# Large two-operand work moved from GpSimd to VectorE, and a new order in a mixer and in four layer norms

## The chip, the core and the metric

One core of a Trainium2 chip runs a forward pass of a small network in float32. Its engines are named as in the profile: PE (TensorE), with its weight loads as PEld, DVE (VectorE), ACT (ScalarE), POOL (GpSimd) and SP (SyncE, which here only issues DMAs). The metric is the device time of one execution in microseconds, lower is better.

## The reference

The input is one sequence of 256 tokens with 1024 features. The first block has two layers; each is a mixer, a layer norm, a SwiGLU feed-forward (1024 to twice 2816 and back) and a layer norm, with residuals. The second block has two layers with RMS norms: a half feed-forward, a mixer, a half feed-forward. The part around the change, cut:

```python
def layer_norm(x, g, b):
    mu = jnp.mean(xf, axis=-1, keepdims=True)
    xc = xf - mu
    var = jnp.mean(xc * xc, axis=-1, keepdims=True)
    return xc * lax.rsqrt(var + EPS) * g + b
...
for layer in range(DEPTH):
    ...   # mixer: layer 0 hgrn2 + forgetting attention, layer 1 rg_lru + stick-breaking attention
    x = layer_norm(ALPHA * x + mix, ln_g[layer, 0], ln_b[layer, 0])
    x = layer_norm(ALPHA * x + swiglu(x, ffn_w13[layer], ffn_w2[layer]), ln_g[layer, 1], ln_b[layer, 1])
```

The second block's mixers are an MLA with a dilated attention, and a sparse attention with a sliding-window one. Their logits get a position bias from a table, plus a mask.

## The kernel before, in words

The activations stay in SBUF with features on partitions. All weights pass once through the chip in **chunks** of 256 columns, in the fixed order of `chunk_plan` (L72): `fetch` (L429) issues the DMA of a chunk into `raw` on SP, ACT copies it to `wh` in a rounded format, and DVE makes `wl = raw - wh`, each in two halves of 128x1024. There are 3 `raw`, 4 `wh` and 4 `wl` buffers, so a chunk can be loaded only when an older one's `wl` is made. Activations are split in the same way into `ah` and `al`, and a product is three matmuls: `ah` with `wh`, `ah` with `wl`, `al` with `wh` (`steps_a` L484 gives features on partitions, `steps_b` L505 tokens on partitions). `chunk` (L447) keeps the next three chunks fetched.

In program order: mixer0 (to 143 us in the profile), layer norm 00 (to 174), feed-forward f0 (to 334), layer norm 01 (to 362), mixer1 (to 440), layer norm 10 (to 467), feed-forward f1 (to 626), layer norm 11 (to 655), then h0a (to 835), mixer2 (to 955), h0b (to 1140), h1a (to 1320), mixer3 (to 1430) and h1b.

In a mixer many small chains (attention heads, the levels of `level`, the gated recurrence `lru`) are generators; `weave` (L969) steps them in the order written out in the table `ORDER` (L36), a name per step. Within that a scheduler places the instructions on each engine's own in-order queue. In the layer norms the order is the program's (`manual_schedule`). In mixer0 each of eight `level`s (128 down to 1) makes a 128x1024 tile by two subtractions of 128x512 from the cumulated gates, one by DVE and one by POOL, an exponential on ACT, and two multiplications, again one by DVE and one by POOL.

`ln` (L592) overlaps the norm with the next stage: the un-normalised `x` is already multiplied with the next two weight chunks (`product`), and `first` (L726) corrects the results afterwards. `tail` (called per pair of 128-row blocks) sums x and its squares, `apply` (L735) gets mean and variance from PE, adds minus the mean to x, makes a diagonal of the reciprocal deviations (`dg`), broadcasts it by a matmul with ones (`row`), multiplies x by it, and makes `ah` and `al` of the next stage. `rms` (L794) sums squares in `tot`. In `ffn` (L851), `up` makes gate and up products of a chunk pair and `down` adds the result's share; `LAG` (L59) says by how many pairs `down` trails `up`. `t5_bias` (L1477) loads a bias by SP from a table in DRAM and adds a mask that POOL's queue has loaded. `mixer1.lru` starts with a convolution on DVE.

Every operation of ACT, DVE and POOL is recorded at L337, matmuls at L468, transposes at L481.

Of the kernel before, what the change touches and what calls it, by code (L numbers as in the profile page):

```python
# [12 lines left out]
def _quiet(msg, *args, **kwargs):  # L13
# [11 lines left out]
OP = mybir.AluOpType  # L25
# [12 lines left out]
        qb0 lv16 kb0 lv32 lv64 lv16 lv4 lv1 lv64 qb1 lv128 lv128 kb0 qb0 lv0 qb1 vb0 vb1 lv32 lv1 lv16 kb1 forget lv4  # L38
        lv64 ia0 ia0 fox1 vb0 lv8 lv8 lv0 fox0 vb1 fox1 lv2 lv32 lv1 kb1 fox2 fox3 lv128 fox3 ia1 ga0 ia1 fox1 fox0
        lv2 fox2 ga0 ga1 lv8 fox0 ga1 lv2 lv4 hgrn fox3 fox2 fox0 hgrn hgrn fox2 fox3 fox1 evo0 hgrn evo0 evo0 evo1  # L40
# [18 lines left out]
LAG = {"h0a": 2}  # L59
# [12 lines left out]
def chunk_plan():  # L72
# [25 lines left out]
    for name, c in (("fa", 512), ("qa", 0), ("qb", 2048), ("kb", 2560), ("vb", 3072),  # L98
                    ("ia", 1024), ("ga", 1536)):
        cols(name, "ev_w_in", c, 2)  # L100
# [250 lines left out]
class Net:  # L351
# [132 lines left out]
    def steps_a(s, w, act, n=256, parts=((0, 128), (128, 128))):  # L484
# [4 lines left out]
        for low in range(2):  # L489
            for k in range(8):  # L490

                js = range(len(parts)) if not low or k < 7 else range(len(parts) - 1, -1, -1)
                for j in js:
                    c0, m = parts[j]
                    p, c = o[:m, j * 256:(j + 1) * 256], slice(c0, c0 + m)
                    if low:
                        s.mm(p, h[:, k, c], al[:, k], False, k == 7 and j == 0)
                    else:
                        s.mm(p, h[:, k, c], ah[:, k], k == 0 and j == 0, False)
                        s.mm(p, l[:, k, c], ah[:, k], False, False)  # L500
# [91 lines left out]
    def ln(s, name, ahead=(), gain=None):  # L592
# [79 lines left out]
        def tail(pr, acc):  # L672
# [4 lines left out]
            if pr == 1:  # L677
# [19 lines left out]
            if pr == 3:  # L697
                with manual(ENG.PE):
# [17 lines left out]
                    for n in range(2):  # L716
                        product(n, range(6, 8), low=False)
# [17 lines left out]
        def apply():  # L735
# [21 lines left out]
            for pr in range(2, 4):  # L757
                nc.gpsimd.tensor_tensor(xs[pr], xs[pr], wide(nm), OP.add)
# [1303 lines left out]
```

## Time and profile before

| | us |
|---|---|
| runs timed, median (lowest to highest of 3) | 1635.88 (1635.45 to 1637.84) |
| profiled execution, its own time | 1634.74 |
| its span in the trace | 1633.0 |
| PE busy in the span | 1578.3 (97%) |
| DVE busy | 1098.9 (67%) |
| ACT busy | 850.8 (52%) |
| POOL busy | 214.8 (13%) |
| granted TensorE clock, mean | 0.991 |

The span runs from the first to the last instruction. A matmul's end is modelled and overlaps the next one, so idle time of PE is better read as the wait that the trace puts ahead of an instruction. [...]

### The profile page before, as it was taken

The page shows a single profiled execution, that of the slowest core. Times are in us where ns is not written, and L with a number is a line of the kernel's source. Part 1 is how long each engine was busy: PE and PEld are TensorE (multiplying, and loading weights), DVE is VectorE, ACT ScalarE, POOL GpSimd, SP SyncE. Part 2 cuts the span into 40 slices and gives each one's busy share as a digit, 9 for nine tenths or more (in the row PEclk, how much of TensorE's full clock was granted, in tenths as well). Part 3 has the DMA queues.
Part 4 walks back from the last instruction along what each step waited for, and adds up shares of the span by engine and source line. Part 5 has one row for each costly group of instructions (what it writes and reads, how often), then busy time and mean ns, then how long its engine had stood idle before and what let it go on. Part 6 is the DMA issues. An engine that isn't in the chain of part 4 may idle for free.

```text
span 1633.0 us, 31856 instructions
## 1 busy us (share of the span) xinstructions
PE 1578.3 (97%) x13635; PEld 1537.8 (94%) x13635; DVE 1098.9 (67%) x1683; ACT 850.8 (52%) x1271; POOL 214.8 (13%) x185
## 2 busy tenths in 40 slices
PE   8899999998999999999999999999999999899998
PEld 7798999988999998999999899999999998699998
DVE  7687845499795457856566865556756578775554
ACT  6474644467664445534366754444444456664442
POOL 6313100041120003100033210000000033110000
PEclk9999999999999999999999999999999999999999
DMA  8342655525355552655544435554555546135551
GB/s 302 116 169 78 232 186 202 184 107 181 130 190 217 196 192 104 231 185 204 176 144 156 133 134 195 193 196 166 207 204 183 205 173 225 38 145 199 189 199 60
DMA packets 45057, 282.78 MB, mean 173 GB/s; under 512 B 5170, under 2 KB 9506, under 8 KB 12146
## 3 DMA queue, kind: packets, MB, share of 16 engines
q1 hardware_dynamic: 43376, 277.98, 47.5%
q0 software_dynamic: 1072, 2.50, 0.4%
q8 instruction: 107, 1.75, 0.4%
q10 hardware_dynamic: 468, 0.27, 0.1%
q14 instruction: 34, 0.28, 0.0%
HBM read 279.64 MB, written 1.09 MB: 172 GB/s over the span
## 4 chain that ended last, share of the span: by engine, by line
PE 78%; DVE 13%; ACT 3%; issue 2%; POOL 2%; DMA 1%; ACTq 0%; SPq 0%; DVEq 0%; POOLq 0%
PE p L468 77%; DVE t L337 5%; DVE wl L337 4%; DVE x L337 1%; PE p L481 1%; POOL ts L337 1%; DVE al L337 1%; ACT t L337 1%; DVE ts L337 1%; DMA raw<-in_wst_dram 1%; POOL t L337 1%; ACT wh L337 1%; DVE lp L337 1%; DVE L L337 0%; DMA ident<-in_cst_dram 0%
## 5 line engine op out<-in xcount | busy, mean ns | idle before, releaser
L337 ACT ACTIVATE wh<-raw 128x1024 fp32r<-128x1024 f32 (+1 forms) x517 | 517.6, 1048 | 554.8 <-issue 471.4
L337 DVE TENSOR_TENSOR wl<-raw,wh 128x1024 fp32r<-128x1024 f32 (+1 forms) x517 | 620.8, 1239 | 219.3 <-ACT wh L337 216.6
L468 PE MATMUL p<-ah,wh 128*128 128x256 f32 x2288 | 533.6, 278 | 7.6 <-ACT wh L337 7.2
L468 PE MATMUL p<-ah,wl 128*128 128x256 f32 x2288 | 532.0, 277 | 2.5 <-DVE wl L337 2.0
L468 PE MATMUL p<-t,wh 128*128 128x256 f32 (+1 forms) x2848 | 484.2, 278 | 1.0 <-DVE t L337 0.6
L468 PEld LDWEIGHTS p<-ah,wh 128*128 128x128 f32 x2288 | 431.9, 189 | 8.5 <-ACT wh L337 7.2
L468 PEld LDWEIGHTS p<-ah,wl 128*128 128x128 f32 x2288 | 431.7, 189 | 5.1 <-DVE wl L337 4.9
L468 PEld LDWEIGHTS p<-t,wh 128*128 128x128 f32 x2848 | 421.9, 188 | 5.3 <-ACT t L337 2.4
L468 PE MATMUL p<-t,wl 128*128 128x256 f32 (+1 forms) x1424 | 364.7, 277 | 0.0
L468 PE MATMUL p<-al,wh 128*128 128x256 f32 x2288 | 285.4, 276 | 4.9 <-DVE al L337 4.9
L468 PEld LDWEIGHTS p<-al,wh 128*128 128x128 f32 x2288 | 271.0, 187 | 6.9 <-DVE al L337 6.3
L468 PEld LDWEIGHTS p<-t,wl 128*128 128x128 f32 x1424 | 256.7, 188 | 0.2 <-issue 0.2
L337 DVE TENSOR_TENSOR t<-p,t 128x512 f32<-128x512 f32 (+5 forms) x164 | 97.2, 601 | 183.8 <-PE p L468 180.9
L337 POOL TENSOR_TENSOR t<-t,t 128x512 f32<-128x512 f32 (+1 forms) x35 | 58.7, 1683 | 613.0 <-PE p L468 342.9
L337 ACT ACTIVATE t<-t 128x512 fp32r<-128x512 f32 (+4 forms) x153 | 99.6, 655 | 48.2 <-DVE t L337 47.8
L468 PE MATMUL p<-wh,ah 128*128 128x256 f32 x384 | 112.8, 294 | 3.3 <-ACT wh L337 3.3
L468 PE MATMUL p<-wl,ah 128*128 128x256 f32 x384 | 110.5, 288 | 4.7 <-DVE wl L337 4.7
L337 DVE TENSOR_TENSOR t<-t,t 128x512 fp32r<-128x512 f32 (+3 forms) x148 | 104.4, 710 | 9.8 <-ACT t L337 5.4
L468 PE MATMUL p<-wh,al 128*128 128x256 f32 x384 | 110.4, 288 | 0.0
L337 ACT ACTIVATE t<-p 128x512 f32<-128x512 f32 (+4 forms) x122 | 61.8, 518 | 58.8 <-PE p L468 37.1
L468 PEld LDWEIGHTS p<-wh,ah 128*128 128x128 f32 x384 | 74.1, 193 | 6.3 <-ACT wh L337 3.5
L468 PEld LDWEIGHTS p<-wl,ah 128*128 128x128 f32 x384 | 74.3, 194 | 5.0 <-DVE wl L337 4.9
(167 smaller groups left out, 1071.8 us busy)
## 6 DMA issues: line engine op xcount, KB each, us to landing
raw<-in_wst_dram SPq DMA_DIRECT2D x254, 1024.0 KB, 4.8
t<-table SPq DMA_DIRECT2D x4, 512.0 KB, 8.2
raw<-in_sml_dram SPq DMA_DIRECT2D x2, 1024.0 KB, 5.1
d<-table SPq DMA_DIRECT2D x6, 256.0 KB, 4.4
t<-in_cst_dram POOLq DMA_DIRECT2D x10, 128.0 KB, 4.1
x<-in_xt_dram SPq DMA_DIRECT2D x4, 256.0 KB, 6.8
raw<-in_wst_dram SPq DMA_DIRECT2D x4, 256.0 KB, 6.2
out_dram<-x SPq DMA_DIRECT2D x4, 256.0 KB, 2.2
```

What stands on the lines that cost most here:

```text
L337: return fn(out, *args, **kw)
L468: s.nc.tensor.matmul(o, l, r, start=start, stop=stop)
L481: s.nc.tensor.transpose(o, i, s.flip if back else s.ident[:k, :k])
```

## The change

It moves about 70 two-operand operations on tiles of 128x256 and more from POOL to DVE: the sums of the layer norms and of `rms`, the two `x + nm` of pairs 2 and 3, sixteen operations in `level`, one multiplication in `lru` (its square goes to ACT), and ten mask additions in `t5_bias`. The table for mixer0 is rewritten, and its chunks now come by halves of heads. In the layer norms the diagonal is made after the first `x + nm`, its matmul stands ahead of the last eight early products, and the `wl`, `al` and `first` work on DVE is reordered. The second pair of `up` in f0, f1 and h0a runs by `steps_two`, which uses `al` last. `LAG` of f0 and f1 becomes 2. The chunks `qd` use their `wl` later within `steps_a`.

```diff
 ORDER = {
     "0": """
-        qb0 lv16 kb0 lv32 lv64 lv16 lv4 lv1 lv64 qb1 lv128 lv128 kb0 qb0 lv0 qb1 vb0 vb1 lv32 lv1 lv16 kb1 forget lv4
...
+        qb0 lv16 qb0 lv32 lv64 lv16 kb0 lv4 lv1 kb0 lv64 lv128 vb0 lv128 lv0 vb0 vb1 forget lv32 vb1 lv1 lv16 qb1 lv4 qb1
...
-LAG = {"h0a": 2}
+LAG = {"f0": 2, "f1": 2, "h0a": 2}
...
-    for name, c in (("fa", 512), ("qa", 0), ("qb", 2048), ("kb", 2560), ("vb", 3072),
-                    ("ia", 1024), ("ga", 1536)):
-        cols(name, "ev_w_in", c, 2)
+    for name, c in (("fa0", 512), ("fa1", 768), ("qa0", 0), ("qa1", 256), ("qb0", 2048), ("kb0", 2560), ("vb0", 3072), ("vb1", 3328),
+                    ("qb1", 2304), ("kb1", 2816), ("ia0", 1024), ("ia1", 1280), ("ga0", 1536), ("ga1", 1792)):
+        a(name, "ev_w_in", 0, c)
...
-    def steps_a(s, w, act, n=256, parts=((0, 128), (128, 128))):
+    def steps_a(s, w, act, n=256, parts=((0, 128), (128, 128)), early=False):
...
-        for low in range(2):
+        for low in (0, 2, 1) if early else (0, 1):
...
-                    if low:
+                    if low == 1:
                         s.mm(p, h[:, k, c], al[:, k], False, k == 7 and j == 0)
-                    else:
+                    if low == 0:
                         s.mm(p, h[:, k, c], ah[:, k], k == 0 and j == 0, False)
+                    if low == 2 or not (low or early):
                         s.mm(p, l[:, k, c], ah[:, k], False, False)
...
+    def steps_two(s, ws, act):
+        ws = [[a.rearrange("p (k c) -> p k c", c=256) for a in w] for w in ws]
+        ah, al = act
+        os = [s.ps() for _ in ws]
+        def go(o, w, a, k, first=False, last=False):
+            for j in (0, 1) if not (last and k == 7) else (1, 0):
+                s.mm(o[:, j * 256:(j + 1) * 256], w[:, k, j * 128:(j + 1) * 128], a[:, k], first and k == 0 and j == 0, last and k == 7 and j == 0)
+        for k in range(8):
+            for o, w in zip(os, ws):
+                go(o, w[0], ah, k, first=True)
+        for o, w in zip(os, ws):
+            for k in range(8):
+                go(o, w[1], ah, k)
+        for k in range(8):
+            for o, w in zip(os, ws):
+                go(o, w[0], al, k, last=True)
+        return os
     def steps_b(s, w, act):
...
-                nc.gpsimd.tensor_tensor(sums[0], xs[0], xs[1], OP.add)
-                nc.gpsimd.tensor_tensor(sums[1], sums[1], sq, OP.add)
+                nc.vector.tensor_tensor(sums[0], xs[0], xs[1], OP.add)
+                nc.vector.tensor_tensor(sums[1], sums[1], sq, OP.add)
...
-                nc.gpsimd.tensor_tensor(sums[0], sums[0], xs[2], OP.add)
+                nc.vector.tensor_tensor(sums[0], sums[0], xs[2], OP.add)
                 lo(0, 1)
-                halves(nc.gpsimd, half[0], sums[0])
...
+                    halves(nc.vector, half[0], sums[0])
                     add(half[0], xs[3])
                     halves(nc.vector, half[1], sums[1])
                     add(half[1], sq)
-                    lo(2, 3, 4, 5)
+                    lo(2, 3)
                     product(0, range(6), low=False)
                     product(1, range(3), low=False)
...
                     for i in range(4):
                         s.mm(mom[:, 256 + i:257 + i], half[i // 2][:, i % 2 * 128:i % 2 * 128 + 128], s.mean_w[:, 0:1], False, i == 3)
                     product(1, range(3, 6), low=False)
-                    for n in range(2):
-                        product(n, range(6, 8), low=False)
+                    product(0, range(6, 8), low=False)
...
-            lo(6, 7)
-            for pr in range(2):
-                nc.vector.tensor_tensor(xs[pr], xs[pr], wide(nm), OP.add)
+            scaled = lambda pr: nc.vector.tensor_tensor(xs[pr], xs[pr], wide(rr), OP.mult)
+            moved = lambda pr: nc.vector.tensor_tensor(xs[pr], xs[pr], wide(nm), OP.add)
+            moved(0)
             dg = s.T("t1", [128, 2, 128])
             eye = s.ident.rearrange("p (o c) -> p o c", o=1).to_broadcast([128, 2, 128])
             nc.vector.tensor_tensor(dg, eye, rs.rearrange("p (t o) -> p t o", o=1).to_broadcast([128, 2, 128]), OP.mult)
             row = s.ps()
             s.mm(row[:, :256], s.ones, dg.rearrange("p a b -> p (a b)"), True, True)
             nc.scalar.activation(rr, row[:, :256], AF.Copy)
-            for pr in range(2, 4):
-                nc.gpsimd.tensor_tensor(xs[pr], xs[pr], wide(nm), OP.add)
-            next(step, bool)()
-            for n in range(2):
-                product(n, range(8), high=False)
+            product(1, range(6, 8), low=False)
+            moved(1)
+            lo(4, 5)
+            scaled(0)
+            lo(6, 7)
+            scaled(1)
+            for ks in (range(4), range(4, 8)):
+                for n in range(2):
+                    product(n, ks, high=False)
+            for pr in (2, 3):
+                moved(pr)
+                scaled(pr)
             act = s.new_act()
             gd = lambda d: dict(bias=s.v("lnb" + name, d), scale=s.v("lng" + name, d))
             hd = (lambda d: dict(bias=gb[:, 1, d:d + 1], scale=gb[:, 0, d:d + 1])) if gain else gd
-            for pr in range(4):
-                nc.vector.tensor_tensor(xs[pr], xs[pr], wide(rr), OP.mult)
-                for d in (2 * pr, 2 * pr + 1):
-                    nc.scalar.activation(act[0][:, d], s.x[:, d], AF.Identity, **hd(d))
-            next(step, bool)()
-            nc.vector.tensor_tensor(mr, nm, rr, OP.mult)
-            ys = [first(0, rr, mr)] if ahead else []
+            for d in range(8):
+                nc.scalar.activation(act[0][:, d], s.x[:, d], AF.Identity, **hd(d))
+            for late in step:
+                late()
+            mixer = ahead and ahead[0][0] == "x"
+            ys = []
+            if mixer:
+                nc.vector.tensor_tensor(mr, nm, rr, OP.mult)
+                ys = [first(n, rr, mr) for n in range(2)]
...
-            for late in step:
-                late()
             s.pinned = 2
-            if ahead:
+            if mixer:
                 s.late = s.fetch(s.at + 3)
-                ys.append(first(1, rr, mr))
+            elif ahead:
+                for late in s.fetch(s.at + 3):
+                    late()
+                nc.vector.tensor_tensor(mr, nm, rr, OP.mult)
+                ys = [first(n, rr, mr) for n in range(2)]
             return act, ys
...
-                nc.gpsimd.tensor_tensor(tot, tot, sq, OP.add)
+                nc.vector.tensor_tensor(tot, tot, sq, OP.add)
...
         def up(j, ws="gu"):
             if early and j == 1 and ws == "gu":
-                steps = [s.steps_a(s.chunk(f"{pre}{w}{j}"), act) for w in ws]
-                for p in steps:
-                    next(p)
-                for w, p in zip(ws, steps):
-                    try:
-                        next(p)
-                    except StopIteration as e:
-                        made[w, j] = pair(e.value)
-                        if after:
-                            after.pop(0)()
+                for w, o in zip(ws, s.steps_two([s.chunk(f"{pre}{w}{j}") for w in ws], act)):
+                    made[w, j] = pair(o)
+                    if after:
+                        after.pop(0)()
                 return
             for w in ws:
...
-                nc.gpsimd.tensor_tensor(wv[:, :, 0], ref, bv[:, :, 0], OP.subtract)
+                nc.vector.tensor_tensor(wv[:, :, 0], ref, bv[:, :, 0], OP.subtract)
...
-                nc.gpsimd.tensor_tensor(wv[:, :, 0], wv[:, :, 0], kv[:, :, 0], OP.mult)
+                nc.vector.tensor_tensor(wv[:, :, 0], wv[:, :, 0], kv[:, :, 0], OP.mult)
...
-            nc.gpsimd.tensor_tensor(ii, ii, xc, OP.mult)
+            nc.vector.tensor_tensor(ii, ii, xc, OP.mult)
...
-            nc.gpsimd.tensor_tensor(xc, aa, aa, OP.mult)
+            nc.scalar.activation(xc, aa, AF.Square)
...
-                p = (yield from s.steps_a(s.chunk(f"{name}{j}"), act)).rearrange("p (a b) -> p a b", a=2)
+                p = (yield from s.steps_a(s.chunk(f"{name}{j}"), act, early=name == "qd")).rearrange("p (a b) -> p a b", a=2)
...
-        s.nc.gpsimd.tensor_tensor(t, t, mask.rearrange("p (o c) -> p o c", o=1).to_broadcast([128, n, 256]), OP.add)
+        s.nc.vector.tensor_tensor(t, t, mask.rearrange("p (o c) -> p o c", o=1).to_broadcast([128, n, 256]), OP.add)
```

How the queues move, at three places. In mixer0 on DVE, from the eighth chunk's `wl` (wl_453) on; t4 tiles are levels, 314 the cumulated gates, 316 and 168 queries and keys. Before:

```order
L337 TENSOR_TENSOR wl_453<-raw_450,wh_452 128x1024 x2
L337 TENSOR_TENSOR t4_491<-t4_491,t4_316 128x32x16
L337 TENSOR_TENSOR t4_554<-t4_314 128x128x4
L337 TENSOR_TENSOR t4_558<-t4_314 128x512
L337 TENSOR_TENSOR t4_548<-t4_548,t4_316 128x8x64
L337 TENSOR_TENSOR t4_597<-t4_314 128x4x128
L337 TENSOR_TENSOR t4_544<-t4_544,t4_316 128x16x32
L337 TENSOR_TENSOR t4_558<-t4_558,t4_316 128x512
L337 TENSOR_TENSOR ts2_789<-ts2_786,ts2_788 128x64
L337 TENSOR_TENSOR t4_597<-t4_597,t4_316 128x4x128
L337 TENSOR_TENSOR t4_554<-t4_554,t4_316 128x128x4
L337 TENSOR_TENSOR wl_498<-raw_495,wh_497 128x1024 x2
```

and now:

```order
L337 TENSOR_TENSOR wl_453<-raw_450,wh_452 128x1024 x2
L337 TENSOR_TENSOR t4_513<-t4_314 128x16x32
L337 TENSOR_TENSOR t4_517<-t4_314 128x8x64 x2
L337 TENSOR_TENSOR t4_491<-t4_491,t4_316 128x32x16
L337 TENSOR_TENSOR t4_491<-t4_491,t4_168 128x32x16
L337 TENSOR_TENSOR t4_564<-t4_314 128x128x4 x2
L337 TENSOR_TENSOR t4_568<-t4_314 128x512
L337 TENSOR_TENSOR wl_526<-raw_523,wh_525 128x1024 x2
L337 TENSOR_TENSOR t4_568<-t4_314 128x512
L337 TENSOR_TENSOR t4_517<-t4_517,t4_316 128x8x64
L337 TENSOR_TENSOR t4_517<-t4_517,t4_168 128x8x64
L337 TENSOR_TENSOR t4_592<-t4_314 128x4x128 x2
```

Nine level operations stood between the `wl` of the eighth and the ninth chunk, the other half of each level on POOL; now eight do, POOL has none, and the ninth chunk is another (the second half of `qb`). PE's 337th matmul used the ninth chunk before (`vb0`, wh_497 and wl_498); now it uses the eighth (wh_452, wl_453), and the ninth from the 425th on.

On DVE in layer norm 00, from the copy of mean and variance; x is the activation, t the mean and the broadcast row, ident the diagonal's matrix. Before:

```order
L337 COPY ts<-p 128x4
L337 SCALAR_TENSOR_TENSOR ts<-ts 128x2 x2
L337 SCALAR_TENSOR_TENSOR t_1689<-x,ts,t_1688 128x256 x2
L337 TENSOR_TENSOR x<-x,t_1875 128x512 x2
L337 TENSOR_TENSOR t_1883<-ident,ts 128x256
L337 TENSOR_TENSOR wl<-raw,wh 128x1024
L337 TENSOR_TENSOR x<-x,t_1876 128x512 x4
L337 TENSOR_TENSOR wl<-raw,wh 128x1024
```

and now:

```order
L337 COPY ts<-p 128x4
L337 SCALAR_TENSOR_TENSOR ts<-ts 128x2 x2
L337 TENSOR_TENSOR x<-x,t_1865 128x512
L337 TENSOR_TENSOR t_1870<-ident,ts 128x256
L337 TENSOR_TENSOR x<-x,t_1865 128x512
L337 SCALAR_TENSOR_TENSOR t_1689<-x,ts,t_1688 128x256 x2
L337 TENSOR_TENSOR x<-x,t_1866 128x512
L337 SCALAR_TENSOR_TENSOR t_1689<-x,ts,t_1688 128x256 x2
L337 TENSOR_TENSOR x<-x,t_1866 128x512
L337 TENSOR_TENSOR x<-x,t_1865 128x512
L337 TENSOR_TENSOR x<-x,t_1866 128x512
L337 TENSOR_TENSOR x<-x,t_1865 128x512
```

The diagonal moves ahead of one `x + nm` and of the low parts (t_1689), which now stand between the operations on x.

On DVE at the start of h0a, the end of `first` and what follows it, after the change; t_7396 is `tot` of `rms`. Before, its three additions were POOL's.

```order
L337 TENSOR_TENSOR t_7386<-p,t_7279 128x256
L337 TENSOR_TENSOR t_7396<-t_7396,t_7398 128x512
L337 SCALAR_TENSOR_TENSOR t_7386<-t_7280,ts,t_7386 128x256
L337 TENSOR_TENSOR t_7396<-t_7396,t_7401 128x512
L337 TENSOR_TENSOR t_7396<-t_7396,t_7404 128x512
L337 TENSOR_TENSOR wl<-raw,wh 128x1024 x4
L337 TENSOR_SCALAR ts<-p 128x2
L337 TENSOR_TENSOR wl<-raw,wh 128x1024
L337 TENSOR_SCALAR t_7538<-ident,ts 128x128 x2
```

The sums stand behind all of the layer norm's work on DVE, and the next four halves of `wl` between them and the row's diagonal (t_7538).

## Rows read from the trace of the kernel before

**Rows 1.** Page, part 1: each engine's busy time, share of the span, instructions.
```profile
PE 1578.3 (97%) x13635; PEld 1537.8 (94%) x13635; DVE 1098.9 (67%) x1683; ACT 850.8 (52%) x1271; POOL 214.8 (13%) x185
```
**Rows 2.** Waits of PE: who for what, us in total, times, longest.
```profile
PE p L468 <- ACT wh L337: 10.4, 2, 7.2
PE p L468 <- DVE t L337: 9.3, 9, 2.5
```
**Rows 3.** Stretches: us, busy of PE, PEld, DVE, ACT, POOL (instructions); clock, DMA, GB/s.
```profile
58.00:61.50 3.50, 3.49 (x16) 3.49 (x17) 3.50 (x4) 3.15 (x5) 0.00 (x0) 0.51 0.43 98
...
841.00:850.00 9.00, 8.96 (x42) 8.67 (x43) 4.33 (x14) 5.12 (x10) 2.33 (x2) 0.62 0.23 96
...
160.00:174.00 14.00, 11.75 (x95) 11.10 (x93) 13.86 (x21) 9.27 (x19) 7.16 (x6) 1.00 0.21 76
174.00:335.00 161.00, 161.00 (x1411) 160.50 (x1412) 92.12 (x99) 71.16 (x84) 0.00 (x0) 1.00 0.58 210
...
455.00:467.00 12.00, 10.20 (x80) 9.41 (x79) 11.80 (x18) 9.89 (x18) 7.71 (x6) 1.00 0.50 153
628.00:675.00 47.00, 41.52 (x342) 40.16 (x341) 45.03 (x73) 29.65 (x49) 20.21 (x15) 1.00 0.36 135
```
**Rows 4.** Timeline of PE: start, us, operation, in brackets idle before and releaser.
```profile
52.97 0.39 PE L468 MATMUL p<-wh,ah 128*128 128x256 f32 x1 [3.26 <-ACT wh L337]
58.01 0.58 PE L468 MATMUL p<-wl,ah 128*128 128x256 f32 x1 [4.66 <-DVE wl L337]
...
163.01 0.70 PE L468 MATMUL p<-t,ones 128*128 128x256 f32 x2 [1.74 <-DVE t L337]
...
376.73 1.97 PE L468 MATMUL p<-t,t 128*128 128x256 f32 x8 [2.03 <-DVE t L337]
...
643.37 0.70 PE L468 MATMUL p<-t,ones 128*128 128x256 f32 x2 [2.49 <-DVE t L337]
...
841.04 1.05 PE L468 MATMUL p<-ones,t 128*128 128x1 f32 x8 [2.52 <-ACT t L337]
...
962.39 0.78 PE L468 MATMUL p<-al,wh 128*128 128x256 f32 x3 [1.39 <-DVE al L337]
```
**Rows 5.** Timeline of POOL in the same columns.
```profile
48.55 6.99 POOL L337 TENSOR_TENSOR t<-t,t 128x512 f32<-128x512 f32 x4
...
159.41 3.27 POOL L337 TENSOR_TENSOR x<-x,t 128x512 f32<-128x512 f32 x2
...
654.29 5.94 POOL L337 TENSOR_TENSOR t<-t,t 128x512 f32<-128x512 f32 x3 [3.85 <-ACT t L337]
...
840.62 1.50 POOL L337 TENSOR_TENSOR d<-d,t 128x512 f32<-128x512 f32 x1 [2.78 <-DMA t<-in_cst_dram]
...
1336.49 4.94 POOL L337 TENSOR_TENSOR t<-t,t 128x1024 f32<-128x1024 f32 x2 [3.49 <-DMA t<-in_cst_dram]
...
1365.69 2.38 POOL L337 TENSOR_TENSOR t<-t,t 128x1024 f32<-128x1024 f32 x1 [3.16 <-DMA t<-in_cst_dram]
```
**Rows 6.** Timeline of DVE in the same columns.
```profile
30.75 7.14 DVE L337 TENSOR_TENSOR wl<-raw,wh 128x1024 fp32r<-128x1024 f32 x4
...
47.61 1.53 DVE L337 TENSOR_TENSOR t<-t,t 128x512 f32<-128x512 f32 x1
...
56.74 6.89 DVE L337 TENSOR_TENSOR wl<-raw,wh 128x1024 fp32r<-128x1024 f32 x6
...
73.13 0.47 DVE L337 TENSOR_SCALAR t<-p,vec 8x256 f32<-8x256 f32 x1 [5.78 <-PE p L468]
...
159.17 2.38 DVE L337 TENSOR_TENSOR x<-x,t 128x512 f32<-128x512 f32 x2
161.48 1.48 DVE L337 TENSOR_TENSOR t<-ident,ts 128x256 f32<-128x256 f32 x1
...
164.16 2.50 DVE L337 TENSOR_TENSOR x<-x,t 128x512 f32<-128x512 f32 x4
...
658.99 8.00 DVE L337 TENSOR_TENSOR wl<-raw,wh 128x1024 fp32r<-128x1024 f32 x6
666.91 0.15 DVE L337 TENSOR_SCALAR ts<-p 128x2 f32<-128x2 f32 x1
...
835.15 3.78 DVE L337 TENSOR_TENSOR wl<-raw,wh 128x1024 fp32r<-128x1024 f32 x1 [2.59 <-ACT wh L337]
```
**Rows 7.** One tile class, 70 to 90 us: DMAs that bring the forget rows back.
```profile
L337 ACTq DMA_DIRECT2D t<-rows x2: 221/221/221, 79.9 to 83.0; - x2
```

More of the change, by code (lines that the diff above doesn't have):

```diff
@@ L37 @@
     "0": """
-        qb0 lv16 kb0 lv32 lv64 lv16 lv4 lv1 lv64 qb1 lv128 lv128 kb0 qb0 lv0 qb1 vb0 vb1 lv32 lv1 lv16 kb1 forget lv4
-        lv64 ia0 ia0 fox1 vb0 lv8 lv8 lv0 fox0 vb1 fox1 lv2 lv32 lv1 kb1 fox2 fox3 lv128 fox3 ia1 ga0 ia1 fox1 fox0
-        lv2 fox2 ga0 ga1 lv8 fox0 ga1 lv2 lv4 hgrn fox3 fox2 fox0 hgrn hgrn fox2 fox3 fox1 evo0 hgrn evo0 evo0 evo1
+        qb0 lv16 qb0 lv32 lv64 lv16 kb0 lv4 lv1 kb0 lv64 lv128 vb0 lv128 lv0 vb0 vb1 forget lv32 vb1 lv1 lv16 qb1 lv4 qb1
+        lv64 kb1 lv8 lv8 lv0 kb1 fox1 fox0 ia0 fox1 lv2 lv32 lv1 ia0 ia1 lv128 lv2 lv8 ia1 ga0 fox1 fox0 fox2 lv2 lv4 fox3
+        ga0 ga1 fox0 fox2 fox3 ga1 hgrn fox0 hgrn fox2 fox3 hgrn fox1 evo0 hgrn fox2 fox3 evo0 evo0 evo1
         evo1 evo1 evo2 evo2""".split(),
@@ L488, in steps_a @@
         o = s.ps()
-        for low in range(2):
+        for low in (0, 2, 1) if early else (0, 1):
             for k in range(8):
-                js = range(len(parts)) if not low or k < 7 else range(len(parts) - 1, -1, -1)
+                js = range(len(parts)) if low != 1 or k < 7 else range(len(parts) - 1, -1, -1)
                 for j in js:
```

## The prediction

> **What bounds the kernel now.** Start with the page's busy times: PE works in 97% of the span and nothing else comes near [rows 1], and the change adds and removes no matmul of weight. So the time can only fall where PE waits, or runs slow. In a feed-forward stretch it does neither: 161.00 of 161.00 us are busy, 1411 matmuls, one every 0.114 us [rows 3]. The larger `LAG` of f0 and f1 and the order of `up` inside such a stretch are therefore worth nothing: work hides them, and the cover that could go is only the next chunk's arrival.
>
> Next, who PE waits for: ACT's `wh` twice, 10.4 us, and DVE's tiles, 9.3 us in nine waits [rows 2]. The timeline of PE says where [rows 4]. [...]
>
> Last, why DVE is late there. Four `wl` took 7.14 us, 1.78 each, while POOL worked on two-operand tiles; six later ones took 6.89, 1.15 each [rows 6]. A 128x512 operation took 1.53 us beside POOL's four of 6.99 us [rows 5, 6], and 0.62 in a group of four at 164 us when POOL was not at such work [rows 6]. At 835 us a single `wl` took 3.78. I read this as DVE and POOL holding each other up when both read two large operands.
>
> **The change part by part**, against the profiled execution's own 1634.74 us, which is 1.14 below the median of the runs, 1635.88.
>
> *mixer0.* Removed: two waits of PE, 3.26 and 4.66 us, and 1.75 us of half clock behind them [rows 3, 4], together 9.7. Moved: sixteen POOL operations. From 30.75 us DVE now does two chunks' `wl` (four at 1.15, 4.6), three level operations at 0.62, and the eighth chunk's two `wl` (2.3): 39.5 us. PE wants that chunk at about 49.5 us, where it stopped before (52.97 less 3.26). Eight level operations (5.0) and two `wl` (2.3) later, at 46.8, the ninth is there, wanted only 88 matmuls on. Even 0.3 us more on each operation leaves both in time. Both waits go. Late next is the forget chain: its first DVE row now stands behind all levels, at about 59.5 us by the same prices; from that row (73.13) to the last DMA that brings the rows back (83.0, plus its landing, which I put at 2 us from POOL's 2.78 us wait for a small load [rows 5]) it was 12 us [rows 6, 7], so 71.5. PE comes to the heads that need it near 72, so this costs 0 to 2. I take -9.0; between -4 and -9.7.
>
> *Layer norm 00.* PE waited 1.74 us for the diagonal [rows 4]: DVE made it behind two `x + nm` that took 2.38 beside POOL's 3.27, and itself took 1.48 [rows 5, 6]. Now it follows one uncontended `x + nm` (0.62) and the reciprocal, and PE gets there 8 matmuls (0.9 us) sooner. Of PE's 2.25 idle us in 160 to 174 [rows 3] I take all. Added on DVE: three sums and two `x + nm` at 0.62 and a half sum at 0.35, 3.5 us. Two of the sums lie under the projection's matmuls. The half sum now stands ahead of the mean's matmul, +0.2. So -2.0.
>
> [...] DVE is busy 13.86 of 14 us in this stretch, 11.80 of 12 at 455, 45.03 of 47 at 628 [rows 3]: in the layer norms it is DVE that is full, and it gets more. If nothing but its busy time counted, the stage would grow by the 3.5 us added less 2.0 regained (2.38 back to 1.25 for two, 1.48 back to about 0.6): +1.5 in place of -2.0, which is rival A. [...]
>
> *Layer norm 10* has 1.80 us idle in 455 to 467 [rows 3], waits for `wl` and `al`. `steps_two` asks for both 32 matmuls later (3.65 us); they go: -1.6 after the half sum. *Layer norm 01 and mixer1*: PE waited 2.03 us at 376.73 for the convolution on DVE [rows 4], which keeps its place behind the same `wl`. What PE gains earlier it waits there. One 128x1024 product added on DVE (1.2) is off that path. -1.0, between -3 and +1.5.
>
> *Layer norm 11 and h0a.* The diagonal's 2.49 us [rows 4] go as above. But `tot` is now summed on DVE behind the `wl`, `al` and `first` work. POOL had it ready at 660.2 (654.29 + 5.94) [rows 5]; walking DVE's new queue at the prices above gives 662, and PE, ahead by the 5.48 idle us of 628 to 675 [rows 3] without the last wait of some 1.6, asks at 656.5: a wait of 5.5 us. And the scale's row on DVE, at 666.91 behind six `wl` [rows 6], cannot come sooner, as four `wl` and it still follow `tot`. What is gained is waited out, and a wait of that length was followed by half clock at 58 us: 0 to +1.8. I take +1.0.
>
> *mixer2.* The `wl` of 3.78 becomes 1.15, and PE's wait of 2.52 us at 841.04, at the end of the chain behind it, goes; 42 matmuls at clock 0.62 behind it [rows 3, 4] give back up to 3.4. Against that the third mask addition on DVE now waits for its DMA, which POOL did 2.78 us [rows 5]. -3.5, between -6 and +0.5. *h0b*: the `al` wait of 1.39 [rows 4] stood behind a slowed `wl`: -1.4, and no more than that. *mixer3*: four mask additions of 128x1024 at 1.2 on DVE, where POOL waited 3.49 and 3.16 us for masks [rows 5]; DVE comes there about when they land. +1.0, between -2 and +4. The sums of the other norms lie between `tail`s, at 0.62 in gaps of over 2 us of PE work: 0, bound +2.
>
> Sum: -9.0 - 2.0 - 1.6 - 1.0 + 1.0 - 3.5 - 1.4 + 1.0 = -16.5. That is 1618.2 for the profiled execution, and 1619.4 as a median.
>
> **The rivals.** *A: DVE takes it back in the layer norms.* For: it is full there. Against: the same operations are slowed by POOL now. Layer norms 00, 10 and 11 at +1.5, +1.9, +2.5, mixer1 +1, the rest as above: -9.0 + 6.9 - 3.5 - 1.4 + 1.0 + 1.0 (other norms) = -5, 1631.
>
> *B, slower: DVE's in-order queue waits for the masks.* A mask addition that waited on POOL held nobody up; on DVE every `wl` and softmax behind it waits too. POOL's three waits were 2.78, 3.49 and 3.16, 9.4 together [rows 5]. If each reaches PE whole, with 1.75 us of half clock behind it, that is +14.7; if the sums for h0a also cost 5.5 + 1.75, and two others 3 each, +13.3. With -9.0 - 2.0 - 1.6 - 1.0 kept, +14.4: 1650. It decides once these waits pass 13.6 us together. Against it: DVE reaches these rows late, and PE has other chunks to work on.
>
> *C: the two engines do not hold each other up*, and the long DVE times have another cause. Then the moved work stays near 1.5 us each: the tenth chunk's `wl` comes some 10 us later than I count, mixer0 keeps half, and the rest is eaten: 1635, no change. Against it: the durations follow POOL's work closely in both directions.
>
> **How the numbers follow.** My forecast 0.72, A 0.14, B 0.08, C 0.06. Alone, the forecast spans 1608 (all lower ends, 1610, and 2 us for short slow stretches that I have not priced) to 1629 (mixer0 and mixer2, the widest terms, at their upper ends, +5 and +4). The range for 8 in 10 adds A: 1608 to 1632. About 0.2%, 3.3 us, is what a measurement of this kernel can tell from no change. Faster: the forecast and most of A, 0.84; same: a little of A, most of C, 0.07; slower: B and the rest, 0.09.
>
> **What would show it.** Right: no PE wait over 1 us between 45 and 60 us and clock 1 there; `wl` at 1.15 us throughout; no wait ahead of the ones matmul in the norms; PE waiting about 5 us for `tot` near 655. Wrong: `wl` still at 1.8 us in mixer0 (C); DVE full and PE waiting for `al` after the norms (A); DVE idle ahead of a mask addition with `wl` behind it (B).

## The result, and the profile after

The changed kernel takes 1617.29 us (median of 4 runs, 1616.28 to 1619.36) beside 1636.86 for the kernel before in the same comparison (4 runs, 1635.45 to 1643.76): a ratio of 0.9874, interval 0.9844 to 0.9904. It is faster, by 19.6 us where 16.5 were forecast. The page of the profiled execution (1616.28 us), its first lines:

```profile
span 1614.5 us, 31806 instructions
...
PE 1570.6 (97%) x13635; PEld 1535.5 (95%) x13635; DVE 1092.6 (68%) x1752; ACT 851.1 (53%) x1272; POOL 118.7 (7%) x115
```

DVE executes 69 instructions more than in [rows 1] and is busy for 6.3 us less; POOL loses 70 instructions and 96 us. The stretch of mixer0 in which the two waits lay, and two stretches of [rows 3] at the same place of the program, which the changed kernel reaches 8 to 15 us earlier:

```profile
44.00:60.00 16.00, 16.00 (x151) 15.23 (x151) 15.72 (x22) 10.16 (x13) 0.00 (x0) 1.00 0.48 169
...
151.00:163.00 12.00, 12.00 (x102) 11.86 (x101) 11.93 (x17) 8.22 (x15) 8.37 (x5) 1.00 0.10 23
...
613.00:662.00 49.00, 42.08 (x337) 41.56 (x336) 44.56 (x82) 28.59 (x47) 11.10 (x6) 0.93 0.36 134
```

In mixer0 and in layer norm 00 PE now never stands still and the granted clock, which the profile gives as a share of full speed, is 1.00; in layer norm 00 that is with DVE as full as before (11.93 of 12). Around layer norm 11 it is worse: the same work takes some 49 us instead of 47, at a clock of 0.93 instead of 1.00. Who PE waits for, in the waits of the changed kernel (us in total, times, longest):

```profile
PE p L468 <- DVE t L337: 9.8, 6, 6.4
...
PE p L481 <- DVE t L337: 7.8, 5, 2.8
PE p L468 <- ACT wh L337: 7.1, 1, 7.1
...
PE p L481 <- DVE ts L337: 6.9, 2, 6.6
...
PE p L468 <- DVE al L337: 2.9, 1, 2.9
```

The first line has a single wait of 6.4 us in it that the kernel before has not [rows 2]. PE's timeline shows it, with the other waits that the steps of the prediction speak of:

```profile
351.18 4.42 PE L468 MATMUL p<-al,wh 128*128 128x256 f32 x23 [2.91 <-DVE al L337]
...
364.03 1.97 PE L468 MATMUL p<-t,t 128*128 128x256 f32 x8 [1.17 <-DVE t L337]
...
403.70 1.82 PE L481 MATMUL p<-ident,t 128*128 128x128 f32 x12 [2.83 <-DVE t L337]
...
646.48 1.84 PE L468 MATMUL p<-ones,t 128*128 128x1 f32 x8 [6.39 <-DVE t L337]
...
829.66 0.61 PE L468 MATMUL p<-ones,t 128*128 128x1 f32 x4 [0.35 <-ACT t L337]
...
863.35 1.09 PE L481 MATMUL p<-ident,t 128*128 128x128 f32 x4 [2.43 <-DVE t L337]
```

And DVE's timeline at the same places:

```profile
31.07 4.61 DVE L337 TENSOR_TENSOR wl<-raw,wh 128x1024 fp32r<-128x1024 f32 x4
...
59.26 0.46 DVE L337 TENSOR_SCALAR t<-p,vec 8x256 f32<-8x256 f32 x1
...
151.56 0.42 DVE L337 TENSOR_TENSOR t<-ident,ts 128x256 f32<-128x256 f32 x1
...
644.85 1.48 DVE L337 TENSOR_TENSOR t<-t,t 128x512 f32<-128x512 f32 x2
646.25 4.63 DVE L337 TENSOR_TENSOR wl<-raw,wh 128x1024 fp32r<-128x1024 f32 x4
650.79 0.15 DVE L337 TENSOR_SCALAR ts<-p 128x2 f32<-128x2 f32 x1
...
822.15 1.23 DVE L337 TENSOR_TENSOR wl<-raw,wh 128x1024 fp32r<-128x1024 f32 x1 [2.80 <-ACT wh L337]
...
826.42 0.69 DVE L337 TENSOR_TENSOR d<-d,t 128x512 f32<-128x512 f32 x1 [0.17 <-DMA t<-in_cst_dram]
...
862.51 0.69 DVE L337 TENSOR_TENSOR t<-t,ts 128x512 f32<-128x512 f32 x1 [1.53 <-POOL ts L337]
...
1318.45 2.36 DVE L337 TENSOR_TENSOR t<-t,t 128x1024 f32<-128x1024 f32 x2
```

A `wl` is at 1.15 us now (4.61 for four at 31.07, 1.23 alone at 822.15) where [rows 6] had 1.78 and 3.78, and none of the 517 takes over 1.42; the diagonal takes 0.42 instead of 1.48; the third mask addition of mixer2 waits 0.17 us for its DMA.

Both kernels issue the same 13635 matmuls, so the starts of the k-th matmul in the two traces can be subtracted. The table gives, for each stage, by how many us that difference changes; the stages are named by the times of the kernel before. The small matmuls that some experiments add are left out of the count. Two experiments, told below, stand beside it.

| stage (us of before) | forecast | changed kernel | order alone | moves alone |
|---|---|---|---|---|
| start, to 45 | - | +1.0 | +1.1 | +0.9 |
| mixer0, to 143 | -9.0 | -9.1 | -9.1 | -8.6 |
| layer norm 00, to 174 | -2.0 | -2.9 | -3.0 | -1.0 |
| f0, to 330 | 0 | -0.4 | +0.8 | 0.0 |
| layer norm 01, to 362 | -1.0 with mixer1 | -4.0 | -2.9 | -1.0 |
| mixer1, to 440 | | +3.5 | +3.2 | +2.3 |
| layer norm 10, to 480 | -1.6 | -3.1 | -1.9 | -0.8 |
| f1, to 620 | 0 | 0.0 | 0.0 | 0.0 |
| layer norm 11 and h0a's start, to 680 | +1.0 | +2.0 | +1.7 | 0.0 |
| mixer2, 836 to 960 | -3.5 | -1.2 | +1.5 | -0.5 |
| h0b's start, to 970 | -1.4 | -1.9 | +3.2 | -1.9 |
| mixer3, 1318 to 1430 | +1.0 | -2.2 | +0.3 | -2.3 |
| rest | - | -0.2 | 0.0 | -0.3 |
| last matmul | -16.5 | -18.5 | -4.9 | -13.2 |

### The profile page after: what moved, and what is told of

The parts are those of the page before. It is cut to its first block, busy times and chain, and to the rows that moved or that the text cites. A ratio compares the mean times of both kernels' runs of the same rounds, so it can differ in the third digit from the quotient of the medians.

```text
span 1614.5 us, 31806 instructions
## 1 busy us (share of the span) xinstructions
PE 1570.6 (97%) x13635; PEld 1535.5 (95%) x13635; DVE 1092.6 (68%) x1752; ACT 851.1 (53%) x1272; POOL 118.7 (7%) x115
## 3 DMA queue, kind: packets, MB, share of 16 engines
q8 instruction: 107, 1.75, 0.4%
## 5 line engine op out<-in xcount | busy, mean ns | idle before, releaser
L337 DVE TENSOR_TENSOR wl<-raw,wh 128x1024 fp32r<-128x1024 f32 (+1 forms) x517 | 609.0, 1216 | 219.3 <-ACT wh L337 219.1
L468 PE MATMUL p<-ah,wh 128*128 128x256 f32 x2288 | 519.8, 278 | 7.9 <-ACT wh L337 7.1
L468 PE MATMUL p<-ah,wl 128*128 128x256 f32 x2288 | 517.6, 277 | 0.3
L468 PEld LDWEIGHTS p<-ah,wh 128*128 128x128 f32 x2288 | 423.4, 189 | 9.3 <-ACT wh L337 7.1
L468 PEld LDWEIGHTS p<-ah,wl 128*128 128x128 f32 x2288 | 423.0, 189 | 1.3 <-DVE wl L337 0.9
L337 DVE TENSOR_TENSOR t<-t,t 128x512 f32<-128x512 f32 (+3 forms) x183 | 122.9, 680 | 10.4 <-ACT t L337 5.7
L337 ACT ACTIVATE t<-t 128x512 fp32r<-128x512 f32 (+5 forms) x154 | 100.7, 657 | 33.7 <-DVE t L337 33.4
L337 POOL TENSOR_TENSOR ts<-ts,mhalf 128x2 f32<-128x2 f32 (+4 forms) x29 | 46.8, 1612 | 956.4 <-DVE ts L337 956.4
```

The costliest lines, as they stand in the source:

```text
L337: return fn(out, *args, **kw)
L468: s.nc.tensor.matmul(o, l, r, start=start, stop=stop)
```

## The experiments

The theory: POOL's two-operand work slows DVE's, and taking it away, with the new order, removes PE's waits and the half clock behind them (0.51 over 58 to 61.5 us in [rows 3]). Rivals are a saturated DVE that takes it back, engines that don't hold each other up, and waits in DVE's queue for masks.

### Order alone, moves alone

`e1_moves_back` keeps the new order and gives all the moved operations to POOL again; `e2_moves_only` is the kernel before with nothing but the same engine changes, in the other direction.

```diff
-                nc.vector.tensor_tensor(sums[0], xs[0], xs[1], OP.add)
+                nc.gpsimd.tensor_tensor(sums[0], xs[0], xs[1], OP.add)
...
-                nc.vector.tensor_tensor(wv[:, :, 0], ref, bv[:, :, 0], OP.subtract)
+                nc.gpsimd.tensor_tensor(wv[:, :, 0], ref, bv[:, :, 0], OP.subtract)
...
-            nc.scalar.activation(xc, aa, AF.Square)
+            nc.gpsimd.tensor_tensor(xc, aa, aa, OP.mult)
```

> The changed kernel with all moved operations back on POOL; the new orders stay. My theory (the two engines hold each other up, and the new order matters by itself in mixer0): wl beside POOL's work is back at 1.6 to 1.8 us, mixer0 keeps most of its gain because PE's next chunk stands earlier in DVE's queue, the layer norms lose 2 to 3 us each, h0a's wait for tot (6.4 us) goes. About 1625, between 1620 and 1632. Rival, order alone makes the gain: 1617 within 3. Rival, moves alone make it: 1634 or more.

> The kernel before with only the moves (POOL to DVE, one square to ACT); all orders as before. My theory: wl at 1.15 us everywhere, but in mixer0 eighteen level operations stand on DVE ahead of the ninth chunk's wl, 11 us at 0.62, where nine at about 1.55 took 14; so a wait of about 5 us stays there, with half clock behind it; the norms gain 1 each, mixer2 1. About 1628, between 1622 and 1636. Rival, moves alone make the gain: 1617 within 3. Rival, order alone: 1636 or slower, since DVE has 50 us more to do.

Measured: order alone 1626.94 us (4 runs, ratio 0.9939, 0.9924 to 0.9955), moves alone 1621.74 (4 runs, 0.9901, 0.9882 to 0.9919), each against 1637.93 (7 runs). The first lies in its range, the second just below it, as the wait of some 5 us expected in mixer0 is far shorter. DVE's timeline with the order alone:

```profile
31.65 7.14 DVE L337 TENSOR_TENSOR wl<-raw,wh 128x1024 fp32r<-128x1024 f32 x4
...
41.37 2.35 DVE L337 TENSOR_TENSOR wl<-raw,wh 128x1024 fp32r<-128x1024 f32 x2
```

Four `wl` are back at 1.78 us each, and still mixer0 keeps all of its gain: the eighth chunk's `wl` is ready at 43.7 us, and PE comes to it at 51.0, with its 337th matmul. With the moves alone it is the other way round. PE's timeline there:

```profile
51.79 0.39 PE L468 MATMUL p<-wl,ah 128*128 128x256 f32 x1 [1.05 <-DVE wl L337]
```

The old order stays, and eighteen level operations, POOL's share among them, stand ahead of the ninth chunk; but at 0.62 us each they leave PE a wait of only 1.05 us. So in mixer0 each half of the change is enough by itself (-9.1 and -8.6); the two don't add. The halves' gains, 11.0 and 16.2 us as medians, sum to more than the 19.6 of both.

Two steps of the theory on e1 fell. The layer norms were to lose 2 to 3 us each with POOL back; 00 lost nothing, 01 and 10 lost 1.1 and 1.2. And the wait in layer norm 11 was to go with the sum on POOL; it split in two, and the stage stays at +1.7. PE's timeline of e1:

```profile
646.38 1.05 PE L468 MATMUL p<-ones,t 128*128 128x1 f32 x8 [2.58 <-POOL t L337]
...
657.49 0.67 PE L468 MATMUL p<-t,ones 128*128 128x256 f32 x2 [2.89 <-DVE t L337]
```

The +1.5 and +3.2 of the order alone in mixer2 and at h0b's start are not shown to be its doing: e10, below, which has the code of the kernel before there, shows +2.3 and +3.1 (see the last section).

### POOL's work put where it harms nobody

`e3_pool_load` adds five POOL operations of 128x512 to three pairs of each of two feed-forwards, two-operand ones in f0 and one-operand ones in f1; nobody reads what they write.

```diff
+            if pre in ("f0", "f1") and j in (3, 5, 7):
+                o = s.T("t4", [128, 2, 256])
+                for _ in range(5):
+                    if pre == "f0":
+                        nc.gpsimd.tensor_tensor(o, g, s.x[:, 0:2], OP.add)
+                    else:
+                        nc.gpsimd.tensor_scalar(o, g, 0.5, None, OP.mult)
```

> The changed kernel with idle POOL given work that nobody uses: in f0, at three of eleven pairs, five additions of two 128x512 tiles in SBUF; in f1 at the same places five operations on one 128x512 tile and a constant. My theory: beside the additions a wl on DVE takes 1.6 to 1.8 us in place of 1.15, and the additions take 1.6 or more; beside the one-operand work less, 1.2 to 1.4. PE loses under 1 us, since DVE has slack there. Rival C of the prediction: wl stays at 1.15 in both.

Measured: 1616.24 us, one run; no stage of PE behind the start moved by more than 0.12 us. DVE's timeline, first four around a load in f0, then two beside a load in f1:

```profile
224.00 2.36 DVE L337 TENSOR_TENSOR wl<-raw,wh 128x1024 fp32r<-128x1024 f32 x2 [3.19 <-ACT wh L337]
...
228.37 0.69 DVE L337 TENSOR_TENSOR t<-p,t 128x512 f32<-128x512 f32 x1 [2.01 <-PE p L468]
229.45 4.16 DVE L337 TENSOR_TENSOR wl<-raw,wh 128x1024 fp32r<-128x1024 f32 x2 [0.39 <-ACT wh L337]
233.52 1.80 DVE L337 TENSOR_TENSOR t<-t,t 128x512 fp32r<-128x512 f32 x1
...
518.52 3.19 DVE L337 TENSOR_TENSOR wl<-raw,wh 128x1024 fp32r<-128x1024 f32 x2 [0.38 <-ACT wh L337]
521.63 1.12 DVE L337 TENSOR_TENSOR t<-t,t 128x512 fp32r<-128x512 f32 x1
```

POOL worked from 225.48 to 234.8 us. Inside that, two `wl` take 4.16 instead of 2.36, a 128x512 with both operands in SBUF 1.80 instead of 0.69, and one whose first operand is in PSUM (`p`) takes 0.69 (at 228.37), as it does at 212.05 with POOL idle. Beside one-operand work of POOL the `wl` and the 128x512 in SBUF take 3.19 and 1.12. Beside the additions that is more than the 1.6 to 1.8 expected of a `wl`. It is rival C's end: the durations follow POOL's work, put there on purpose. Taken singly, DVE, POOL, DVE:

```profile
229.45 1.92 DVE L337 TENSOR_TENSOR wl<-raw,wh 128x1024 fp32r<-128x1024 f32 x1 [0.39 <-ACT wh L337]
230.36 2.16 POOL L337 TENSOR_TENSOR t<-t,x 128x512 f32<-128x512 f32 x1
231.28 2.32 DVE L337 TENSOR_TENSOR wl<-raw,wh 128x1024 fp32r<-128x1024 f32 x1
```

They end at 231.37, 232.52 and 233.60 us, 1.1 to 1.2 us apart, about what each takes alone (1.21 for a `wl` at 235.24 here, 1.29 for an addition of 128x512 at 928.03 us in the kernel before, where DVE stands still): in these rows the two engines end in turns, an instruction each. Beside the one-operand work the lengthening is smaller: two `wl` from 518.52 take 0.83 us more than the 2.36 alone, with POOL at work throughout (five operations from 514.55, 8.53 us together); beside the additions it is 1.80 more. Why the instruction with an operand in PSUM is spared, and why one-operand work costs less, is not shown; the rows give durations.

### The early sum for h0a on PE

`e4_tot_pe` leaves out DVE's additions into `tot` at the start of h0a: the four squares are kept, and the matmuls with ones sum them.

```diff
+            if given:
+                sq = tot if pr == 0 else s.T("t2", [128, 2, 256])
+                nc.scalar.activation(sq, xs, AF.Square)
+                squares.append(sq)
...
-                for d in range(2):
-                    s.mm(ss[:, t:t + 1], tot[:, d, t * 128:(t + 1) * 128], s.one, d == 0, d == 1)
+                for n, (q, d) in enumerate(parts):
+                    s.mm(ss[:, t:t + 1], q[:, d, t * 128:(t + 1) * 128], s.one, n == 0, n == len(parts) - 1)
```

> The changed kernel with the squares of h0a's norm summed by PE (16 small matmul calls in place of 4) and not by three additions on DVE. My theory: PE's wait of 6.4 us near 640 us goes, 24 small matmuls of 0.13 us more cost 3.1: 1614, between 1612 and 1616. Rival, the row behind it binds anyway: no change, 1617 within 1.

Measured: 1616.59 us (4 runs, 0.9871, 0.9856 to 0.9887). The median lies above the range, where the rival had it, but the stage of layer norm 11 goes from +2.0 to -1.4: 3.4 us less, what the theory had (6.4 less 3.1). PE's timeline:

```profile
640.78 0.50 PE L468 MATMUL p<-ones,t 128*128 128x1 f32 x4
...
643.65 2.49 PE L468 MATMUL p<-ones,t 128*128 128x1 f32 x20
```

The wait of 6.39 us is gone; over 640 to 660 us the granted clock is 0.91 instead of 0.83, and PE has 144 matmuls in it, 24 of them the added small ones, instead of 97. The median falls by only 0.7 us all the same: in the profiled run mixer1 lost 1.7 us at a place that the edit doesn't touch (see the last section), and the timed runs spread over 4 us. That this stage had 3.4 us in it is shown; that the kernel is faster by them is not.

### What the larger LAG and `steps_two` are worth

The prediction gave both nothing within a feed-forward. `e6_lag1` takes the new `LAG` away from the changed kernel, `e10_lag_only` gives it to the kernel before, `e8_up_old` puts the old loop in the place of `steps_two`.

```diff
-LAG = {"f0": 2, "f1": 2, "h0a": 2}
+LAG = {"h0a": 2}
```

> The changed kernel with f0 and f1 trailing by one pair again. My theory: inside f0 and f1 PE is busy without a gap, so nothing changes: 1616 within 1 of the changed kernel's profiled run. Rival: with one pair less ahead, the first down waits for the product of gate and up, 1 to 3 us in f0 and in f1.

> The kernel before with only the larger LAG of f0 and f1. My theory after e6: LAG 2 pays only where first is late, as in the changed kernel; before, f0 and f1 ran without a gap, so nothing changes: 1637 within 2. Rival: LAG 2 is worth 8 us in each feed-forward by itself: 1621.

> The changed kernel with the second pair of up as before (no steps_two), so that PE wants al 32 matmuls, 3.6 us, earlier. My theory: DVE makes al only 2 to 3 us after that, as wl stands ahead of it, so PE waits 2 to 3.6 us for al in layer norms 00 and 10; in 11 the wait for tot hides it. 4 to 7 us above the changed kernel, about 1622. Rival: the moves alone make al early enough: within 1.

Measured, one run each: e6 1637.23 us, 20 above the changed kernel, e10 1637.66 beside 1638.64 for before (9 runs), e8 1625.89. The theory on e6 fell entirely: against the changed kernel f0 loses 8.0 us near its start and f1 8.3. PE's timeline in e6, the window around it in e6 and in the changed kernel, and DVE's end of `first` in e6:

```profile
173.30 6.03 PE L468 MATMUL p<-t,wh 128*128 128x256 f32 x32 [5.63 <-ACT t L337]
```

```profile
160.00:174.00 14.00, 8.37 (x71) 8.17 (x70) 13.21 (x27) 5.64 (x10) 3.27 (x2) 0.89 0.60 225
```

```profile
160.00:174.00 14.00, 14.00 (x126) 14.00 (x125) 13.93 (x27) 7.68 (x13) 4.03 (x2) 1.00 0.59 226
```

```profile
172.11 0.47 DVE L337 SCALAR_TENSOR_TENSOR t<-t,ts,t 128x256 f32<-128x256 f32 x1
```

`first`, which makes the first pair's products whole, now stands behind all of the norm's work on DVE and ends at 172.6 us. The first `down` needs it through ACT, and with a lag of one pair that `down` comes too soon: PE waits 5.63 us and has 71 matmuls in the window where the changed kernel, 0.8 us behind it in the program, has 126. With a lag of two a further pair of `up` covers it. In the kernel before, where `first` was early, the same lag is worth nothing (e10). e8 took 9.6 us more than the changed kernel's profiled run: 5.8 of them in layer norms 00 and 10, where I had expected waits for `al`, and 2.3 in mixer1, which the edit doesn't touch; PE's timeline there and the window show another tile and the clock:

```profile
159.90 0.39 PE L468 MATMUL p<-ah,wl 128*128 128x256 f32 x1 [1.86 <-DVE wl L337]
```

```profile
159.00:164.00 5.00, 4.10 (x21) 4.11 (x22) 5.00 (x6) 4.70 (x8) 5.00 (x2) 0.66 0.36 108
```

The old loop asks for `wl` after its first two matmuls, and DVE is only then making it. PE waits 1.86 us, and the granted clock over 159 to 164 us is 0.66. `steps_two` asks for `wl` 32 matmuls later, so part of what the layer norms gain is its doing.

### The masks, and the best version

`e5_bias_pool` gives only the mask additions back to POOL. `e7_x_act` is e4 with the scalings of x in a norm that POOL still did on ACT. `e9_best` is e7 with mixer2's six mask additions on POOL.

```diff
-        s.nc.vector.tensor_tensor(t, t, mask.rearrange("p (o c) -> p o c", o=1).to_broadcast([128, n, 256]), OP.add)
+        s.nc.gpsimd.tensor_tensor(t, t, mask.rearrange("p (o c) -> p o c", o=1).to_broadcast([128, n, 256]), OP.add)
```

```diff
-            for d in (4, 5, 6, 7):
+            for d in range(8):
...
-            for d in range(4):
-                nc.gpsimd.tensor_scalar(s.x[:, d], s.x[:, d], gd(d)["scale"], gd(d)["bias"], OP.mult, OP.add)
-            for pr in (0, 2, 1, 3):
+            for pr in range(4):
```

> The changed kernel with only the ten mask additions back on POOL. My theory: in mixer2 the early gain of 4.9 us goes (a wl beside POOL's additions takes 3.8 again and its chain is late), and so do the waits of 2.6 and three of 0.8 to 1.0 us that took most of it back; mixer2 within 1.5 of the changed kernel's, mixer3 loses its 2.2. About 1619, between 1616 and 1621. Rival: the additions on DVE are what takes mixer2's gain back; without them it stays, 1614.

> The kernel of e4 with the four scalings of x that each layer norm still has on POOL moved to ACT. My theory: they are one-operand work that slows DVE's wl, al and x operations by 5 to 10 per cent (4.82 for four wl, 4.61 elsewhere); DVE gets 0.5 to 1 us per norm back and ACT has 2.1 us more to do per norm: 1 to 3 us below e4 at best. Rival: ACT's wh come 2.1 us later and PE waits for them: 1 to 4 us above e4.

> The kernel of e7 with mixer2's six mask additions back on POOL; mixer3's four stay on DVE. My theory (additions on DVE take mixer2's gain back, in mixer3 they save 1.5): 3 us below e7, 1611, between 1609 and 1613. Rival: in e5 it was chance where the additions fell beside DVE's work; here a wl meets them again: 1614 to 1616.

Measured: e5 1619.84 us (4 runs, 1617.3 to 1626.01; ratio 0.9904, 0.9877 to 0.993); e7 1614.15 (4 runs, 1613.24 to 1614.72; 0.9856, 0.984 to 0.9871); e9 1613.46 (5 runs, 1612.59 to 1618.32; 0.9852, 0.9837 to 0.9868). As times e5 and the changed kernel can't be told apart, since their intervals overlap. In e5's profile mixer2 is 3.0 us better than in the changed kernel, not within 1.5 of it as the theory had it, and mixer3 1.6 worse, which looked as if the additions of mixer2 belonged on POOL. e9 put them there, and the theory fell. Its DVE, POOL and PE there:

```profile
819.45 3.78 DVE L337 TENSOR_TENSOR wl<-raw,wh 128x1024 fp32r<-128x1024 f32 x1 [2.80 <-ACT wh L337]
```

```profile
819.60 2.53 POOL L337 TENSOR_TENSOR d<-d,t 128x512 f32<-128x512 f32 x2
```

```profile
825.34 1.05 PE L468 MATMUL p<-ones,t 128*128 128x1 f32 x8 [2.52 <-ACT t L337]
```

These are the 3.78 and the 2.52 us of the kernel before [rows 4, 6], to the hundredth. In e5 POOL's addition happened to wait for its mask until the `wl` (824.67 to 825.90 us) was nearly done:

```profile
825.47 2.82 POOL L337 TENSOR_TENSOR d<-d,t 128x512 f32<-128x512 f32 x2 [0.66 <-DMA t<-in_cst_dram]
```

So e5's gain there hung on when a DMA landed. What e7 was to free came: in layer norm 00 five operations on x take 3.35 us instead of 3.74, four `wl` 4.62 instead of 4.82 and four `al` 2.48 instead of 2.69, 0.8 together. As a time it is not clear of e4's, whose interval overlaps. e7 and e9 are equal within the measurement. All of e7's runs lie below all of the changed kernel's, by 3.1 us in the median, but they ran on another chip and the intervals of the two ratios overlap: probably faster, not shown.

## Why the prediction was right, and where its steps were not

- **mixer0: right**, -9.1 for -9.0, by the mechanism named. Of the waits' 9.7 us, 1.75 were put down to half clock; [rows 3] have 16 matmuls in 3.49 us at a granted clock of 0.51, 0.218 each, where f0's take 0.114 at 1.00, which makes 1.66. No wait of PE is left between 44 and 60 us, the clock there is 1.00, `wl` is at 1.15, and the forget chain's first DVE row starts at 59.26 where 59.5 was worked out. What the prediction didn't see is that order and moves each would have sufficed.
- **Layer norms 00 and 10: right, under-sized**, -2.9 and -3.1 for -2.0 and -1.6. The diagonal did what was said. Rival A fell: DVE stays full (11.93 of 12) and PE doesn't wait. Shorter operations are only part of the reason: with the moved work back on POOL (e1) layer norm 00 still has -3.0 and 10 -1.9, so the new order and the cover for what is late do most of it there; the moves alone give -1.0 and -0.8.
- **The step that failed in its reason: that the larger `LAG` of f0 and f1 and the order of `up` inside a feed-forward "are therefore worth nothing".** By e6, `LAG` pays 8 us at the start of f0 and of f1; it is the cover for a `first` that the change itself made late. By e8, `steps_two` pays 3.8 and 2.0 in layer norms 00 and 10, as cover for a late `wl`; the prediction had counted on it in 10, but not in 00. The sum was unhurt only by luck: the late `first` had not been costed either, so that two errors of the same size cancelled.
- **Layer norm 01 and mixer1: right together**, -0.5 for -1.0. What the norm gained (4.0) was waited out in mixer1, but not only at the convolution (1.17 us where [rows 4] had 2.03): 2.91 us go to `al` at 351.18, and 2.83 to a tile of DVE at 403.70.
- **Layer norm 11 and h0a: right in kind**, +2.0 for +1.0, just above its 0 to +1.8. PE waits 6.39 us where 5.5 was worked out, for the sum, with slow clock behind it (0.73 over 646 to 656 us). e4 shows that the sum's place on DVE is the cause, as the stage turns to -1.4 with the sum on PE; with the sum, and all else, back on POOL (e1) it stays at +1.7.
- **mixer2: the mis-sized term**, -1.2 for -3.5. The forecast gain came (the `wl` at 1.23, PE's wait at 829.66 down to 0.35, -4.9 in all), and 3.7 were given back, 2.43 of them as a new wait for DVE at 863.35. That tile (862.51 on DVE) waits for a small operation of POOL, which starts 5.05 us after DVE's `L<-L,ts` (854.88). It does so in all seven kernels with mixer2's mask additions on DVE, and 2.04 us after it in the five with them on POOL, where the scheduler puts less of DVE's work between the two. So moving the additions cost something here, in DVE's order, and not at their DMAs, where the prediction looked for it. No run changes that order by itself.
- **mixer3: wrong in sign**, -2.2 for +1.0, just outside its -2 to +4. DVE reached the masks after they had landed; the two additions at 1318.45 take 2.36 us with no wait, and with them back on POOL (e5) 1.6 us are lost again. This is also rival B's end: its queue of waits for masks didn't form anywhere (0.17 us at 826.42).
- **h0b: -1.9 for -1.4**, and the moves alone give it.
- **The sum** is nearer (-18.5 for -16.5) than its parts: mixer2 came out 2.3 us worse and mixer3 3.2 better than forecast, which is luck again.

## What to carry to other kernels

Two-operand operations given to GpSimd weren't free in this kernel, though GpSimd was busy for only 13% of the span: a `wl` of VectorE beside them took 1.78 or 3.78 us instead of 1.15 and 1.23, 1.5 to 3.1 times as long, and taking 70 of them back on a VectorE that was full in the layer norms lowered its busy time (1098.9 to 1088.8 us in e2). Look at the durations of one instruction form with and without the other engine at work before calling an engine saturated. And cost the parts of a change together: here the deeper software pipeline, worth nothing alone (e10), paid 8 us in each of two feed-forwards for work that another part made late (e6), so undo each part from the changed kernel as well as adding it to the old one.

## What was not expected of the hardware

The hold-up showed in both directions. POOL's four one-input scalings of 128x256 in layer norm 00 now stand beside DVE's two-operand work; POOL's timeline of the changed kernel:

```profile
154.72 9.32 POOL L337 TENSOR_SCALAR x<-x,vec 128x256 f32<-128x256 f32 x4 [3.63 <-ACT ah L337]
```

Singly they take 1.68 and 1.49 us beside DVE's `x<-x,t`, and 3.09 and 3.09 beside its `wl`. In the kernel before:

```profile
165.60 4.49 POOL L337 TENSOR_SCALAR x<-x,vec 128x256 f32<-128x256 f32 x4 [2.93 <-ACT ah L337]
```

Only the first of these four met DVE's two-operand work for most of its time and took 2.46 us; the other three took 0.56 to 0.79.

And the clock after a short wait was not the same from run to run. At h0b's start, the kernel before and e10, which has the same code there, after waits of 1.39 and 1.24 us for the same tile:

```profile
962.00:972.00 10.00, 9.61 (x80) 9.45 (x81) 7.09 (x11) 4.28 (x5) 1.64 (x1) 1.00 0.80 277
```

```profile
961.00:971.00 10.00, 9.12 (x50) 9.03 (x51) 6.40 (x9) 2.38 (x3) 2.17 (x2) 0.66 0.73 249
```

That is the +3.1 of e10, and e1 has 0.72 over 950 to 962 us, where it starts h0b. At mixer1's start, one window of e7 and one of e9 at the same place of the program, after waits of 1.84 and 1.86 us for the same tile:

```profile
361.00:370.00 9.00, 7.16 (x52) 6.69 (x52) 8.07 (x18) 7.94 (x14) 0.00 (x0) 1.00 0.93 364
```

```profile
360.00:369.00 9.00, 7.14 (x37) 6.22 (x37) 7.09 (x16) 6.12 (x10) 0.00 (x0) 0.81 0.92 367
```

One stays at 1.00 and does 52 matmuls, the other falls to 0.81 and does 37, 2.3 us of difference. These two ran on different chips, but e3 and e4 ran on one: behind the wait that the changed kernel has at 403.70 us, 2.84 and 2.80 us long there, the same 12 transposes took 1.82 and 2.90 us, which is e4's loss in mixer1. Comparisons by stage therefore carry up to some 3 us of chance at such a wait, an estimate from these three differences, and the kernels that ran once (e3, e6, e8, e10) are read for what moved by more, or for the durations of single instructions.
